# Eight transposes per PSUM tile and one copy out of it, in a rotary-embedding and score kernel

## The chip, the cores and the metric

The kernel runs on one core of one Trainium2 chip. The metric is the device time of one execution in microseconds (us). The engines are PE (matmuls and transposes; PEld is its weight load), DVE (vector), ACT (scalar), POOL, and SP, which here only issues transfers. Sixteen DMA engines (so the profile counts them, and its trace has 16 completions for each of the 112 transfers) move data between HBM and the on-chip memory SBUF. PSUM is the memory that PE writes into (`ps` and `bank` in the profile's rows). The tiles that the kernels take there are of 512 or 1024 float32 numbers per partition; I count them in banks of 512 (2 KB).

## The reference

Two tensors `q` and `k` of shape (16 batches, 512 positions, 16 heads, 64) get a rotary embedding, then all scores are formed per batch and head:

```
q_rot = concat([q1*cos - q2*sin, q1*sin + q2*cos])     # k likewise
scores = einsum('bshd,bthd->bsht', q_rot, k_rot)       # (16, 512, 16, 512) float32
```

The input is 67 MB and the output 268 MB.

## The kernel before

Each batch is cut into four slots of 128 positions (C = 4). DVE applies the rotary embedding in place. PE transposes two heads at a time (HP = 8 blocks of 128x128 per slot), since the matmuls of the scores are written with the head dimension along partitions (64x512 operands in the profile's rows). PE then forms the scores of two heads (`scores(i, p)`, p = 0..7), ACT copies each 128x1024 block from PSUM into a staging buffer, and SP stores one 4 MB staging buffer per slot. I call the eight calls of `scores` for one i, with what is mixed in between them, a round.

The part that the change touches is the transposition. Four transposes fill one bank, one copy empties it, and two banks take turns:

```
ps_s_pool = ctx.enter_context(tc.psum_pool(name="ps_s", bufs=3))   # score tiles, 2 banks each
ps_t_pool = ctx.enter_context(tc.psum_pool(name="ps_t", bufs=2))   # transposes, 1 bank each
...
def transposed(which, n, g, copy):
    bank = ps_t_pool.tile([P, 4, P], fp32, tag="ps_t", name="bank")
    for x in range(4):
        ...                                     # cut: choice of src
        nc.tensor.transpose(bank[:, x, :], src, ident)
    ...                                         # cut: choice of dst in qT or kT
    copy(out=dst, in_=src)
```

In the main part (batches 1 to 15) the query halves are transposed after scores 1 and 3 of a round and copied by DVE, the key halves after scores 5 and 6 and copied by ACT. The first part (batch 0) works on units of four heads, so that scores can begin before a whole batch has been loaded. There the order is: early loads, embedding of unit 0, its transposes and copies, first scores, first 1 MB stores, and after score 3 of rounds 0 and 1 the load of a piece of batch 2:

```
for p in range(HP):
    scores(i, p, st)                            # stores 1 MB after p = 1, 3, 5, 7
    ...                                         # cut
    if p == 3 and i < 2:
        load("kq"[i], 2)
```

## Time and profile before

| | before |
|---|---|
| time, median of 6 runs | 801.9 us (801.0 to 802.9) |
| span of the profiled run | 799.2 us |
| bytes moved | 336.17 MB, 421 GB/s mean |
| queue 1, share of 16 engines' span | 98.4% |
| PE busy | 690.9 us (86%) |
| DVE busy | 544.6 us (68%) |
| ACT busy | 561.8 us (70%) |

The row to look at first is that of the transfer queue, not of PE: a queue that fills 98.4% of the span leaves little for anything else to decide. The 86% of PE is a mean over rounds in which it never pauses and rounds in which its scores wait until a staging buffer has been stored (ACT waits 113.9 us for stores in all, PE's scores 70.9 us for ACT). The prediction below shows how that is read.

This is the timeline of the kernel before around its first score (start, duration, engine, line, operation, count; in brackets the idle time before):

```profile
15.16 5.06 PE L155 MATMUL ps<-kT_t,qT_t 64*128 64x512 f32 x12
15.26 0.59 ACT L142 COPY qT_t<-bank 128x512 f32<-128x512 f32 x1 [0.27 <-PE bank L127]
...
20.03 0.35 SPq L165 DMA_DIRECT2D out_dram<-st  x1
...
23.39 0.34 SPq L165 DMA_DIRECT2D out_dram<-st  x1
23.79 0.49 SPq L79 DMA_DIRECT2D k_sb<-in_k_dram  x1
```

The reader is to see that the first score starts at 15.16 us while the second half of the query copy has not even begun, that two stores are issued, at 20.03 and 23.39 us, and that the load of the keys of batch 2 stands behind them at 23.79.

### The profile page before, as it was taken

What the parts mean: (1) busy time and instruction counts of PE and PEld (TensorE: products, weight loads), DVE (VectorE), ACT (ScalarE), POOL (GpSimd) and SP (SyncE); (2) the same over time, 40 slices, a digit from 0 to 9 for tenths busy, and PEclk for the clock granted to TensorE, in tenths of its full rate; (3) what the DMA queues carried; (4) which work ended last, traced back from release to release, by engine and by line L of the source; (5) the groups of instructions that cost most, each with busy time, mean ns of one, the idle gap of its engine ahead of it and who ended that gap; (6) DMA issues with size and microseconds to landing.
All of it is one profiled execution on the core that took longest, in us unless ns stands there. A gap on an engine that the chain in (4) does not pass through costs nothing.

```text
span 799.2 us, 7712 instructions
## 1 busy us (share of the span) xinstructions
PE 690.9 (86%) x3072; PEld 299.7 (37%) x3072; DVE 544.6 (68%) x516; ACT 561.8 (70%) x647; POOL 0.7 (0%) x6
## 2 busy tenths in 40 slices
PE   4989998997979789797897978979789897889970
PEld 2444443443434334343343433434334343334420
DVE  7999987676858568585684866848668586685300
ACT  3878886776848578585775856768567685667870
POOL 0000000000000000000000000000000000000000
PEclk9999999899989899898998989989899898998995
DMA  9999999999999999999999999999999999998995
GB/s 353 420 426 430 431 416 430 426 433 440 424 438 423 428 435 424 442 425 433 427 433 431 432 431 429 433 433 424 426 428 435 433 402 430 438 426 362 429 422 249
DMA packets 17700, 336.17 MB, mean 421 GB/s; under 512 B 1792, under 2 KB 3072, under 8 KB 4096
## 3 DMA queue, kind: packets, MB, share of 16 engines
q1 hardware_dynamic: 17376, 335.55, 98.4%
q8 instruction: 24, 0.39, 0.2%
q10 hardware_dynamic: 288, 0.13, 0.1%
q14 instruction: 12, 0.10, 0.0%
HBM read 67.24 MB, written 268.44 MB: 420 GB/s over the span
## 4 chain that ended last, share of the span: by engine, by line
DMA 50%; PE 37%; DVE 5%; ACT 4%; issue 1%; ACTq 0%; DVEq 0%
DMA out_dram<-st 49%; PE ps L155 28%; PE bank L127 9%; ACT st L162 4%; DVE part L106 2%; DVE early L111 1%; DVE k_sb L107 1%; DVE k_sb L111 1%; DVE early L107 1%; DMA early<-in_k_dram 1%; DVE kT_t L142 0%; DVE q_sb L107 0%; DVE q_sb L111 0%; ACTq L270 0%; DVE qT_t L142 0%
## 5 line engine op out<-in xcount | busy, mean ns | idle before, releaser
L162 ACT COPY st<-ps 128x1024 f32<-128x1024 f32 x512 | 495.3, 1018 | 202.8 <-DMA out_dram<-st 113.9
L155 PE MATMUL ps<-kT_t,qT_t 64*128 64x512 f32 x2048 | 548.6, 654 | 70.9 <-ACT st L162 70.9
L155 PEld LDWEIGHTS ps<-kT_t,qT_t 64*128 64x128 f32 x2048 | 185.4, 198 | 258.9 <-issue 138.9
L142 DVE COPY qT_t<-bank 128x512 f32<-128x512 f32 x118 | 81.6, 691 | 202.4 <-PE bank L127 202.4
L127 PEld LDWEIGHTS bank<-ident,q_sb 128*128 128x128 f32 x480 | 55.6, 152 | 104.5 <-issue 101.9
L127 PE MATMUL bank<-ident,q_sb 128*128 128x128 f32 x480 | 86.8, 309 | 0.9 <-PE ps L155 0.9
L127 PEld LDWEIGHTS bank<-ident,k_sb 128*128 128x128 f32 x480 | 50.5, 141 | 95.1 <-DVE k_sb L107 38.0
L127 PE MATMUL bank<-ident,k_sb 128*128 128x128 f32 x480 | 78.7, 287 | 1.6 <-DVE qT_t L142 1.2
L142 ACT COPY kT_t<-bank 128x512 f32<-128x512 f32 x122 | 72.4, 597 | 6.2 <-PE bank L127 6.2
L107 DVE TENSOR_TENSOR q_sb<-q_sb,cos_t 128x1024 f32<-128x1024 f32 x60 | 73.5, 1225 | 2.1
L111 DVE TENSOR_TENSOR k_sb<-k_sb,part 128x1024 f32<-128x1024 f32 x60 | 73.5, 1225 | 2.1
L107 DVE TENSOR_TENSOR k_sb<-k_sb,cos_t 128x1024 f32<-128x1024 f32 x60 | 73.5, 1225 | 2.0
L106 DVE TENSOR_TENSOR part<-q_sb,ss_t 128x1024 f32<-128x1024 f32 x60 | 73.5, 1225 | 2.0
L106 DVE TENSOR_TENSOR part<-k_sb,ss_t 128x1024 f32<-128x1024 f32 x60 | 73.0, 1216 | 0.1
L111 DVE TENSOR_TENSOR q_sb<-q_sb,part 128x1024 f32<-128x1024 f32 x60 | 72.9, 1216 | 0.0
L127 PE MATMUL bank<-ident,early 128*128 128x128 f32 x64 | 10.5, 316 | 12.2 <-DVE early L111 10.3
L127 PEld LDWEIGHTS bank<-ident,early 128*128 128x128 f32 x64 | 8.3, 161 | 17.6 <-issue 14.3
L106 DVE TENSOR_TENSOR part<-early,ss_t 128x1024 f32<-128x1024 f32 x8 | 9.8, 1223 | 5.7 <-ACT ss_t L187 5.5
L111 DVE TENSOR_TENSOR early<-early,part 128x512 f32<-128x512 f32 x16 | 10.3, 687 | 0.2
L107 DVE TENSOR_TENSOR early<-early,cos_t 128x1024 f32<-128x1024 f32 x8 | 9.8, 1224 | 0.3
L142 ACT COPY qT_t<-bank 128x512 f32<-128x512 f32 x10 | 5.6, 615 | 3.2 <-PE bank L127 3.2
L142 DVE COPY kT_t<-bank 128x512 f32<-128x512 f32 x6 | 4.1, 685 | 1.3 <-PE bank L127 1.3
(9 smaller groups left out, 2.8 us busy)
## 6 DMA issues: line engine op xcount, KB each, us to landing
out_dram<-st SPq DMA_DIRECT2D x60, 4096.0 KB, 25.0
k_sb<-in_k_dram SPq DMA_DIRECT2D x15, 2048.0 KB, 28.4
q_sb<-in_q_dram SPq DMA_DIRECT2D x15, 2048.0 KB, 27.5
out_dram<-st SPq DMA_DIRECT2D x16, 1024.0 KB, 13.0
early<-in_k_dram SPq DMA_DIRECT2D x1, 1536.0 KB, 9.1
early<-in_q_dram SPq DMA_DIRECT2D x1, 1536.0 KB, 12.3
early<-in_k_dram SPq DMA_DIRECT2D x1, 512.0 KB, 4.7
early<-in_q_dram SPq DMA_DIRECT2D x1, 512.0 KB, 5.4
```

Of the source, the lines that this page charges most:

```text
L106: nc.vector.tensor_tensor(pv, xs, ss, op=mult)
L107: nc.vector.tensor_tensor(xc, xc, cs, op=mult)
L111: nc.vector.tensor_tensor(y, y, z, op=add)
L127: nc.tensor.transpose(bank[:, x, :], src, ident)
L142: copy(out=dst, in_=src)
L155: nc.tensor.matmul(out=po, lhsT=lhs[64 * r : 64 * r + 64, :], rhs=rh, start=True, stop=True)
L162: nc.scalar.copy(out=so, in_=si)
```

## The change

All eight transposes of a slot or unit go into one tile of two banks, which one copy empties. The intent is fewer and larger copies, and fewer switches of PE between transposes and scores (in the kernel before, the first score after transposes took 1.06 us, a further one 0.86). The tiles take eight banks as before (now 3 x 2 + 1 x 2); the price is that there is no second transpose tile any more.

```diff
-    ps_t_pool = ctx.enter_context(tc.psum_pool(name="ps_t", bufs=2))
+    ps_t_pool = ctx.enter_context(tc.psum_pool(name="ps_t", bufs=1))
...
-    def transposed(which, n, g, copy):
-        bank = ps_t_pool.tile([P, 4, P], fp32, tag="ps_t", name="bank")
-        for x in range(4):
+    def transposed(which, n, copy):
+        bank = ps_t_pool.tile([P, HP, P], fp32, tag="ps_t", name="bank")
+        for g in range(HP // C):
+            for x in range(C):
...
         # first part, after the scores of a round's p
-                if p in (0, 1) and i > 0:
+                if p == 0 and i > 0:
...
         # main part
-                tr[1], tr[3] = ("q", i + 1, 0), ("q", i + 1, 1)
+                tr[2] = ("q", i + 1)
...
-                tr[5], tr[6] = ("k", i + C, 0), ("k", i + C, 1)
+                tr[5] = ("k", i + C)
```

More of the change, by code (lines that the diff above doesn't have):

```diff
@@ L116 @@
     qT = {}
-    def transposed(which, n, g, copy):
-        bank = ps_t_pool.tile([P, 4, P], fp32, tag="ps_t", name="bank")
-        for x in range(4):
-            if n < C:
-                src = units[which, n][:, x, P * g : P * (g + 1)]
-            else:
-                src = batches[which, n // C][:, n % C, P * (4 * g + x) : P * (4 * g + x + 1)]
-            nc.tensor.transpose(bank[:, x, :], src, ident)
+    def transposed(which, n, copy):
+        bank = ps_t_pool.tile([P, HP, P], fp32, tag="ps_t", name="bank")
+        for g in range(HP // C):
+            for x in range(C):
+                if n < C:
+                    src = units[which, n][:, x, P * g : P * (g + 1)]
+                else:
+                    src = batches[which, n // C][:, n % C, P * (C * g + x) : P * (C * g + x + 1)]
+                nc.tensor.transpose(bank[:, C * g + x, :], src, ident)
         src = bank
         if which == "q":
-            if n not in qT:
-                qT[n] = qt_pool.tile([P, HP, P], fp32, tag="qT", name="qT_t")
-            dst = qT[n][:, 4 * g : 4 * g + 4, :]
+            qT[n] = qt_pool.tile([P, HP, P], fp32, tag="qT", name="qT_t")
+            dst = qT[n]
         else:
@@ L137, in transposed @@
             if n < C:
-                dst = kT[b][:, 2 * n + g].rearrange("p (t c) -> p t c", c=C)
-                src = bank.rearrange("p c t -> p t c")
+                dst = kT[b][:, 2 * n : 2 * n + 2].rearrange("p g (t c) -> p g t c", c=C)
+                src = bank.rearrange("p (g c) t -> p g t c", c=C)
             else:
-                dst = kT[b][:, 4 * g : 4 * g + 4, P * (n % C) : P * (n % C + 1)]
+                dst = kT[b][:, :, P * (n % C) : P * (n % C + 1)]
         copy(out=dst, in_=src)
@@ L167, in scores @@
             nc.sync.dma_start(o_v[b, i % C], st)
-    def tr_act(which, n):
-        for g in range(2):
-            transposed(which, n, g, nc.scalar.copy)
     def run(ops):
@@ L189 @@
             run(rope(which, 0))
-            tr_act(which, 0)
+            transposed(which, 0, nc.scalar.copy)
         for i in range(C):
@@ L202 @@
                 scores(i, p, st)
-                if p in (0, 1) and i > 0:
+                if p == 0 and i > 0:
                     run(dve[:1])
                     dve = dve[1:]
-                    transposed("k", C + i - 1, p, nc.vector.tensor_copy)
+                    transposed("k", C + i - 1, nc.vector.tensor_copy)
                 if p == 3 and i < 2:
@@ L212 @@
                     dve = dve[m:]
-                    tr_act(*nxt.pop(0))
+                    transposed(*nxt.pop(0), nc.scalar.copy)
             run(dve)
```

## The prediction

> **What bounds the kernel now.** I read the page first, then the table of stretches, then the chain that ended last, then the timeline of single rounds. The page's second part shows a kernel whose transfers never rest:
>
> ```profile
> DMA  9999999999999999999999999999999999998995
> GB/s 353 420 426 430 431 416 430 426 433 440 424 438 423 428 435 424 442 425 433 427 433 431 432 431 429 433 433 424 426 428 435 433 402 430 438 426 362 429 422 249
> q1 hardware_dynamic: 17376, 335.55, 98.4%
> ```
>
> The reader is to see that the mean of the 16 DMA engines is at 90% or more in all slices but two, and that queue 1, which carries the kernel's own data, alone fills 98.4% of 16 engines' span: 0.984 x 799.2 = 786 us of the 799 us. The change moves not one byte of these 335.55 MB. In the middle (150 to 600 us) the stretches give a DMA share of 1.00 at 430 to 431 GB/s, so there is no hole there to fill.
>
> Two holes are left, and they decide whether anything can be won. The table of stretches shows them (the columns are the stretch, PE, weight loads, DVE, ACT, POOL with counts, then granted clock, DMA share, GB/s):
>
> ```profile
> 726.00:728.00 2.00, 2.00 (x12) 0.72 (x8) 1.93 (x3) 1.57 (x3) 0.00 (x0) 0.95 0.53 229
> 728.00:730.00 2.00, 2.00 (x12) 1.11 (x12) 1.97 (x2) 1.71 (x4) 0.00 (x0) 1.00 0.34 147
> 730.00:732.00 2.00, 2.00 (x12) 0.81 (x8) 0.06 (x1) 2.00 (x3) 0.00 (x0) 1.00 0.65 279
> ...
> 788.00:790.00 2.00, 0.00 (x0) 0.00 (x0) 0.00 (x0) 0.00 (x0) 0.00 (x0) 0.50 1.22 524
> 790.00:792.00 2.00, 0.00 (x0) 0.00 (x0) 0.00 (x0) 0.00 (x0) 0.00 (x0) 0.50 0.16 66
> 792.00:794.00 2.00, 0.00 (x0) 0.00 (x0) 0.00 (x0) 0.00 (x0) 0.00 (x0) 0.50 0.04 16
> 794.00:796.00 2.00, 0.00 (x0) 0.00 (x0) 0.00 (x0) 0.00 (x0) 0.00 (x0) 0.50 0.08 33
> 796.00:799.00 3.00, 0.00 (x0) 0.00 (x0) 0.00 (x0) 0.00 (x0) 0.00 (x0) 0.50 0.03 11
> ```
>
> In the last 8 us a share of 0.03 to 0.08 is about 1/16 = 0.0625: one engine of the sixteen still works while fifteen are done. The completion records in the trace (sixteen per transfer) agree: the last store completes on the median engine at 790.97 us and on the last engine at 798.33. This laggard falls behind slowly: its distance to the median is 0.7 us at 20 us, 5 us at 340, 10.3 us at 739. A 4 MB store takes the others 9.7 us from one completion to the next and the laggard 9.95; only the last two stores, after every instruction has been fetched, take it 9.69 and 9.67. So I take the bound to be **the slowest DMA engine**, which seems never to be without work. The hole at 726 to 734 is then that of the fifteen fast engines, which had run 10 us ahead; at 728 the laggard still had two stores to do.
>
> The compute engines are fast enough, by little. A steady round (one 4 MB store, a quarter of each input batch, 4.19 + 1.05 = 5.24 MB) needs 5.24 MB / 430 GB/s = 12.2 us of DMA. The timeline shows a round that no transfer holds up, from one transpose to the same one a round later (552.62 to 562.64 us): 10.02 us of PE, which is its slowest engine. So PE idles about 2 us a round, seen as ACT waiting 113.9 us for stores to free a staging buffer (first row below).
>
> ```profile
> L162 ACT COPY st<-ps 128x1024 f32<-128x1024 f32 x512 | 495.3, 1018 | 202.8 <-DMA out_dram<-st 113.9
> L142 DVE COPY qT_t<-bank 128x512 f32<-128x512 f32 x118 | 81.6, 691 | 202.4 <-PE bank L127 202.4
> L142 ACT COPY kT_t<-bank 128x512 f32<-128x512 f32 x122 | 72.4, 597 | 6.2 <-PE bank L127 6.2
> L107 DVE TENSOR_TENSOR q_sb<-q_sb,cos_t 128x1024 f32<-128x1024 f32 x60 | 73.5, 1225 | 2.1
> ```
>
> [...]
>
> **The change part by part.**
> 1. DVE copies. In the main part 59 rounds each lose two copies of 691 ns for one of 1024 elements. The rotary products have that size, at 1225 ns, and cost 687 ns at 512 elements, so I take 1225. Saved: 2 x 691 - 1225 = 157 ns a round, some 9 us of DVE busy time. It lies beside the DMA: 0 on the path.
> 2. ACT copies. About 66 pairs of 597 ns become 66 single ones of about 1020 ns (the score copy is 1018): 174 ns each, 11 us of ACT busy time, but less in pace, since pairs overlap (two in 1.12 us at 48.79). Also beside the DMA.
> 3. PE. In the round above PE spends 8 scores x 0.86 + 4 x 0.20 + 4 x 0.585 = 10.02 us: a score alone is 0.86 and the first after transposes 1.06, from blocks of one score (1.06) and three (2.78). The first part of the kernel shows eight transposes in a row, 20.15 to 21.18 = 1.03 us. After: 8 x 0.86 + 2 x 0.20 + 2 x 1.03 = 9.34, **0.68 us less a round**. Times 60 it is 41 us of PE, but the round waits for 12.2 us of DMA anyway: 0 on the path.
> 4. The lost second buffer. Key transposes start three scores after the query ones end: 3 x 0.86 + 0.20 = 2.8 us. The DVE copy between takes 1.2 us plus about 0.15 of handover. The other way there are five scores, 4.5 us, against one ACT copy of 1.0 and at most a score copy of 1.0 before it. No wait in the steady part; margin 1.4 us.
> 5. Start. The first key and query copies end about 0.4 us later, and the first score, which needed only half of the query copy (15.16 us), now needs all of it: 1.2 us later. The first store would go out at about 21 us, not 20.03. The loads queued before it keep the DMA engines busy until about 24 (last early load complete at 23.7 on the first engine, 24.9 on the last): hidden.
> 6. Instructions. Some 125 copies and their waits disappear. Queues 8 and 14 carry instructions on the same DMA engines; 12 fetches of queue 14 may become 10 or 11, at 0.31 us each: at most 0.6 us, if they lie on the laggard.
>
> Sum on the path: 0 to -0.6 us, estimated as -0.4.
>
> **The rivals.**
> - *The single tile becomes a wait.* If DVE has the rotary products ahead of the query copy (2.45 us a pair), the key transposes could wait, and PE's round grow from 9.34 towards 11. Against it: DVE waits 202.4 us for the transposes (second row above), so it stands ready before the copy. Even a wait of 1.5 us per round stays under 12.2. It would need over 2.9 us in every round to show; then +10 us or more. I give it 2%.
> - *The shorter PE round pays.* After the last load (681 us) a round only stores 4.19 MB, 9.75 us of DMA against 10.02 of PE, so PE is the bound of the fifteen fast engines and the hole at 726 to 734, worth about 3.7 us (shares of 0.53, 0.34, 0.65, 0.63 over 8 us), could close. That would give 798 to 799, still inside 2%. Against it: the laggard has a backlog through the hole, so closing it only lets the fast engines get further ahead.
> - *A later first store leaves the queue empty*: +1 us at most, by item 5.
> - *Run-to-run drift of the laggard.* The three runs before lie within 1.2 us[...].
>
> **Range and chances.** 802.4 - 0.4 = 802.0 us. Below, 800.0 allows for half of the tail hole; above, 804.0 for a bubble at the start and drift. Faster by over 2% would need 16 us out of transfers that fill the span, slower by 2% a wait of 2.9 us each round: faster 0.01, same 0.97, slower 0.02.
>
> **What would show it.** Right: span within 4 us; DMA share 1.00 in the middle; DVE copies about 1225 ns x59, ACT copies about 1020; an unhindered PE round of about 9.3 us; more idle time of ACT on out_dram<-st than 113.9 us, by some tens of us; again about 1/16 of DMA at the end. Wrong: PE rows of the transposes waiting for the copies by tens of us, a DMA share under 0.95 in the middle, or a span some 4 us shorter with no tail of one engine, which would mean that the laggard is not the bound.

Two passages are cut from this text where marked, a paragraph of general statements and a clause on what may move the slowest engine's end: runs and traces of this case do not show them. No term of the sum is cut. It stays at 0 to -0.6 us, estimated as -0.4: items 1 to 5 count as 0 on the path, and item 6 gives at most 0.6 us (two fetches of 0.31 us; ten of the twelve fetches of queue 14 took 309 ns). That fetches take the place of the kernel's own transfers agrees with the packet records: during the 36 fetches of queues 8 and 14 in the kernel before, 15.1 packets of queue 1 are under way on average, and 16.0 in the mean from 150 to 600 us. The last fetch of that trace starts at 765.7 us.

## The result

| | before | after |
|---|---|---|
| time, median of 6 runs | 801.9 us | 802.78 us (802.4 to 804.3) |
| span of the profiled run | 799.2 us | 801.0 us |
| PE busy | 690.9 us | 651.6 us |
| DVE busy | 544.6 us | 540.9 us |
| ACT busy | 561.8 us | 549.7 us |

The ratio of the fast runs is 1.0016, with a 95% interval of 1.0003 to 1.0029. A ratio is the mean time of one kernel's fast runs over that of the other's of the same rounds, so it is not quite the ratio of the medians. The change is the same within 2%, and if anything slower by about 1 us.

The transfers of the changed kernel, from the page's second and third part:

```profile
DMA  9999999999999999999999999999999999998995
GB/s 352 383 426 437 432 415 429 428 429 443 421 439 423 432 430 421 441 423 433 430 427 434 433 430 427 432 432 433 432 431 430 430 406 438 429 433 358 442 420 224
...
q1 hardware_dynamic: 17376, 335.55, 98.3%
```

The bytes and the share are those of before. One number differs early: the second slice (20 to 40 us) has 383 GB/s where the kernel before had 420.

The groups that answer to those of the prediction, in its order and without the rows between them (busy us, mean ns of one, idle before and its releaser):

```profile
L162 ACT COPY st<-ps 128x1024 f32<-128x1024 f32 x512 | 488.9, 1031 | 209.9 <-DMA out_dram<-st 165.4
L142 DVE COPY qT_t<-bank 128x1024 f32<-128x1024 f32 x59 | 72.3, 1225 | 201.0 <-PE bank L128 201.0
L142 ACT COPY kT_t<-bank 128x1024 f32<-128x1024 f32 x61 | 63.5, 1041 | 11.9 <-PE bank L128 11.9
L107 DVE TENSOR_TENSOR q_sb<-q_sb,cos_t 128x1024 f32<-128x1024 f32 x60 | 73.5, 1225 | 2.1
```

The copies became single ones of the expected size and duration, and what was won on the engines reappears in the first row: ACT waits 165.4 us for stores to free a staging buffer, not 113.9.

The end of the changed kernel, in the table of stretches:

```profile
790.00:792.00 2.00, 0.00 (x0) 0.00 (x0) 0.00 (x0) 0.00 (x0) 0.00 (x0) 0.50 0.42 180
792.00:794.00 2.00, 0.00 (x0) 0.00 (x0) 0.00 (x0) 0.00 (x0) 0.00 (x0) 0.50 0.08 33
794.00:796.00 2.00, 0.00 (x0) 0.00 (x0) 0.00 (x0) 0.00 (x0) 0.00 (x0) 0.50 0.04 16
```

Again about one engine in sixteen works through the last 8 us. The last of the sixteen completions of the last store comes at 800.17 us, 1.84 us later than before; the median one comes at 791.54, not 790.97.

**Where the 1.84 us come from.** I compared the last of the sixteen completions of each transfer, changed against before, one trace of each. (The records don't name the engine; in what follows "the slowest engine" is whichever completes last.) Up to 30 us the difference is 0.2 us or less. At the load of the keys of batch 2 it jumps to +1.54 (36.59 against 35.05). It is +1.2 at 51 us, +2.5 at 189 and +2.2 at 209 us, and from there to the end it moves only between 1.5 and 2.2. So the changed kernel is not slower per round. It lost time in the first 210 us, most of it in one jump near 30 us, and never got it back. The timeline of its start shows what is there:

```profile
15.37 1.01 ACT L142 COPY qT_t<-bank 128x1024 f32<-128x1024 f32 x1 [2.84 <-PE bank L128]
...
16.44 5.39 PE L155 MATMUL ps<-kT_t,qT_t 64*128 64x512 f32 x12 [1.10 <-ACT qT_t L142]
...
21.30 0.35 SPq L165 DMA_DIRECT2D out_dram<-st  x1
...
25.00 0.34 SPq L165 DMA_DIRECT2D out_dram<-st  x1
25.39 0.43 SPq L79 DMA_DIRECT2D k_sb<-in_k_dram  x1
```

The first score waits for the whole query copy and starts 1.28 us later, the first store is issued 1.27 us later, the second (25.00 us) and the load behind it 1.6 us later.

Two rows of stretches of 10 us in the first part, of the kernel before:

```profile
26.00:36.00 10.00, 10.00 (x51) 4.53 (x52) 8.60 (x11) 8.69 (x13) 0.00 (x0) 1.00 1.02 422
36.00:46.00 10.00, 9.11 (x50) 4.54 (x50) 9.83 (x11) 7.57 (x11) 0.00 (x0) 1.00 1.03 435
```

and of the changed kernel:

```profile
26.00:36.00 10.00, 9.19 (x52) 4.71 (x50) 6.27 (x8) 7.96 (x9) 0.00 (x0) 1.00 0.98 348
36.00:46.00 10.00, 8.37 (x44) 3.71 (x42) 9.79 (x11) 8.23 (x9) 0.00 (x0) 1.00 1.02 431
```

The last two columns are the DMA share and GB/s. Between 26 and 36 us the changed kernel's DMA engines count as busy (0.98) but move 348 GB/s, not 422: 74 GB/s over 10 us is 0.74 MB, or 1.7 us at 430 GB/s. So little of this is an empty queue (the share fell by 0.04, 0.4 us of the 10). The packets themselves take longer: in the packet records the 16 KB packets of the key load have a mean of 762 ns in the changed kernel and 634 before, the 8 KB packets of the second store 365 and 310.

### The profile page after: what moved, and what is told of

Same layout as the page of the kernel before. It is cut to its first block, busy times and chain, and to the rows that moved or that the text cites. A ratio compares the mean times of both kernels' runs of the same rounds, so it can differ in the third digit from the quotient of the medians.

```text
span 801.0 us, 7596 instructions
## 1 busy us (share of the span) xinstructions
PE 651.6 (81%) x3072; PEld 309.6 (39%) x3072; DVE 540.9 (68%) x454; ACT 549.7 (69%) x581; POOL 0.7 (0%) x6
## 4 chain that ended last, share of the span: by engine, by line
DMA 59%; PE 19%; ACT 13%; DVE 5%; issue 1%; ACTq 0%
DMA out_dram<-st 59%; PE ps L155 15%; ACT st L162 12%; PE bank L128 4%; DVE part L106 2%; ACT kT_t L142 1%; DVE early L111 1%; DVE k_sb L107 1%; DVE k_sb L111 1%; DVE early L107 1%; DMA sin_t<-in_sin_dram 0%; DVE kT_t L142 0%; DVE q_sb L107 0%; DVE q_sb L111 0%; ACT qT_t L142 0%
## 5 line engine op out<-in xcount | busy, mean ns | idle before, releaser
L162 ACT COPY st<-ps 128x1024 f32<-128x1024 f32 x512 | 488.9, 1031 | 209.9 <-DMA out_dram<-st 165.4
L155 PE MATMUL ps<-kT_t,qT_t 64*128 64x512 f32 x2048 | 522.4, 652 | 110.3 <-ACT st L162 108.8
L155 PEld LDWEIGHTS ps<-kT_t,qT_t 64*128 64x128 f32 x2048 | 196.2, 201 | 347.8 <-ACT st L162 206.3
L142 DVE COPY qT_t<-bank 128x1024 f32<-128x1024 f32 x59 | 72.3, 1225 | 201.0 <-PE bank L128 201.0
L106 DVE TENSOR_TENSOR part<-q_sb,ss_t 128x1024 f32<-128x1024 f32 x60 | 73.5, 1225 | 2.1
L107 DVE TENSOR_TENSOR q_sb<-q_sb,cos_t 128x1024 f32<-128x1024 f32 x60 | 73.5, 1225 | 2.1
L111 DVE TENSOR_TENSOR k_sb<-k_sb,part 128x1024 f32<-128x1024 f32 x60 | 73.5, 1225 | 2.1
L107 DVE TENSOR_TENSOR k_sb<-k_sb,cos_t 128x1024 f32<-128x1024 f32 x60 | 73.5, 1225 | 2.1
L106 DVE TENSOR_TENSOR part<-k_sb,ss_t 128x1024 f32<-128x1024 f32 x60 | 73.5, 1225 | 2.0
L142 ACT COPY kT_t<-bank 128x1024 f32<-128x1024 f32 x61 | 63.5, 1041 | 11.9 <-PE bank L128 11.9
L128 PEld LDWEIGHTS bank<-ident,q_sb 128*128 128x128 f32 x480 | 51.3, 140 | 46.9 <-issue 24.2
L128 PE MATMUL bank<-ident,k_sb 128*128 128x128 f32 x480 | 68.0, 286 | 1.4 <-DVE qT_t L142 1.4
L128 PE MATMUL bank<-ident,q_sb 128*128 128x128 f32 x480 | 65.5, 279 | 1.4 <-issue 1.4
L106 DVE TENSOR_TENSOR part<-early,ss_t 128x1024 f32<-128x1024 f32 x8 | 9.8, 1225 | 5.9 <-ACT ss_t L183 5.6
L111 DVE TENSOR_TENSOR early<-early,part 128x512 f32<-128x512 f32 x16 | 10.3, 687 | 0.2
L142 ACT COPY qT_t<-bank 128x1024 f32<-128x1024 f32 x5 | 5.2, 1032 | 4.3 <-PE bank L128 4.3
L142 DVE COPY kT_t<-bank 128x1024 f32<-128x1024 f32 x3 | 3.7, 1220 | 3.6 <-PE bank L128 3.6
```

The source lines that it names most:

```text
L106: nc.vector.tensor_tensor(pv, xs, ss, op=mult)
L107: nc.vector.tensor_tensor(xc, xc, cs, op=mult)
L111: nc.vector.tensor_tensor(y, y, z, op=add)
L128: nc.tensor.transpose(bank[:, C * g + x, :], src, ident)
L155: nc.tensor.matmul(out=po, lhsT=lhs[64 * r : 64 * r + 64, :], rhs=rh, start=True, stop=True)
L162: nc.scalar.copy(out=so, in_=si)
```

## The experiments

**Theory 1**: the later first score makes the first stores and the load behind them late, this costs transfer time near 30 us, and since the slowest DMA engine is never idle again, the loss stays to the end. **Theory 2**: it is run-to-run drift. **Theory 3**: the single tile makes PE wait in the main part. And apart from the 1 to 2 us: is the gain of 0.68 us a round real and merely hidden?

Medians and ratios, all against runs of the kernel before on the same chip:

| run | median us | before, same chip | ratio | 95% interval |
|---|---|---|---|---|
| after_again | 803.39 | 800.81 | 1.0026 | 1.0012 to 1.0040 |
| start_halves | 802.30 | 800.81 | 1.0017 | 1.0004 to 1.0029 |
| early_loads | 801.39 | 800.81 | 1.0004 | 0.9992 to 1.0017 |
| split_last | 808.78 | 800.81 | 1.0095 | 1.0081 to 1.0109 |
| before_half | 663.39 | 801.60 | 0.8275 | 0.8262 to 0.8288 |
| after_half | 626.85 | 801.60 | 0.7817 | 0.7807 to 0.7828 |
| delay_start | 805.71 | 801.60 | 1.0054 | 1.0041 to 1.0066 |
| delay_middle | 803.06 | 801.60 | 1.0020 | 1.0007 to 1.0033 |
| before_late | 802.26 | 801.55 | 1.0008 | 0.9995 to 1.0020 |
| before_early | 802.50 | 801.55 | 1.0011 | 0.9997 to 1.0024 |

### after_again: the changed kernel once more

No edit.

> The changed kernel itself once more, for a second trace and more rounds. Theory 1 (the later first store opens a hole in the transfers between 27 and 36 us, and an engine that is never idle again carries it to the end): ratio to before 1.001 to 1.003, and the stretch 26 to 36 us again well below 420 GB/s (before: about 420). Theory 2 (run-to-run drift of the slowest DMA engine): the ratio interval holds 1.000, and the stretch 26 to 36 us is as in before.

The ratio is 1.0026 and its interval does not hold 1. The second trace again shows a slow stretch:

```profile
26.00:36.00 10.00, 9.19 (x50) 4.55 (x48) 6.02 (x7) 7.96 (x10) 0.00 (x0) 1.00 1.00 342
```

342 GB/s, with a second store issued at 25.34 us. This speaks against drift alone (theory 2).

### start_halves: only unit 0 copied in two halves again

```diff
-        copy(out=dst, in_=src)
+        if n == 0:
+            for g in range(2):
+                ...                  # cut: copy of half g of the two-bank tile
+        else:
+            copy(out=dst, in_=src)
```

> Only the copies of unit 0 leave in two halves again, everything else as changed. Theory 1: first score at about 15.2 us and first store at about 20.0 instead of 21.3, the hole shrinks from about 1.5 us to under 0.5, time 0.8 to 1.5 us under the changed kernel of the same rounds. Theory 2 (drift) or 3 (waits for the single tile in the main part): no difference to the changed kernel, within 0.5 us.

The stretch from 26 to 36 us rose to 388 GB/s, about half of the way back to 422. But the first store was issued at 20.99 us, not at the expected 20.0, and the second at 23.98, so the lateness was undone only in part, and mostly not by the edit. The first half copy of the query began only after all eight transposes (15.48 us; before: 14.41), so the first score came at 16.12 us, 0.3 us earlier than in the changed kernel, not 1.2. The rest came from PE: the pairs of score matmuls start 0.85 us apart in the first microseconds of every trace and 0.43 later, and the moment of the switch differs between executions. The first three scores took 4.68 us here, 5.39 in the changed kernel, 5.06 in the kernel before, 5.49 in after_again and 3.54 in before_early. So the issue of the second store varies whatever the edit: 24.44 to 25.34 us in the six traces that start as the changed kernel does, 21.86 to 23.39 in the three that start as the kernel before does. The two ranges don't meet, so the lateness is the change's, but its 1.6 us is known to about 1 us only.

The median is 1.1 us under that of the changed kernel of the same rounds, in the expected range, but the two sets of runs overlap (801.55 to 803.32 against 802.71 to 803.75). It points the way of theory 1 without settling it.

### early_loads: the loads of batch 2 ahead of the first store

```diff
         load("k", 1)
         load("q", 1)
+        load("k", 2)
+        load("q", 2)
...
-                if p == 3 and i < 2:
-                    load("kq"[i], 2)
```

> The changed kernel with the loads of batch 2 issued right after those of batch 1, so that 4.19 MB more (9.7 us of DMA) stand in the queue ahead of the first store. Theory 1: no stretch of 2 us between 10 and 40 us under 400 GB/s, time 1 to 2 us under the changed kernel, so about 801. Theory 2 or 3: as the changed kernel within 0.5 us.

```profile
26.00:36.00 10.00, 9.19 (x50) 4.74 (x50) 6.26 (x7) 7.96 (x9) 0.00 (x0) 1.00 0.99 419
```

With 4.19 MB more in the queue the slow stretch is gone (419 GB/s), although the first store is issued no earlier (21.20 us). The packets of the loads take 615 ns. All five runs (801.14 to 802.01) lie under all five of the changed kernel (802.71 to 803.75), 2.0 us by the medians, as expected of theory 1. The changed kernel is then level with the kernel before (ratio 1.0004), not ahead of it.

### delay_start and delay_middle: the same delay early and late

```diff
+        if (i, p) == (0, 0):         # delay_middle: (30, 0)
+            for _ in range(4):
+                nc.scalar.copy(out=so, in_=si)
```

> The changed kernel with the first score copied out five times instead of once, so that the first store goes out about 3.7 us later still. Theory 1: what is lost in the start is never won back, so 3 to 4 us slower than the changed kernel, about 806. Rival (the hole is not due to late stores): within 1 us of the changed kernel.

> The same four extra copies, but in round 30, in the steady part. Theory 1: the queue holds 15 us or more of transfers there, so nothing: within 0.7 us of the changed kernel. Rival (any lost time on the evacuating engine counts): 3 to 4 us slower.

The same four extra copies, some 4 us of ACT, cost clearly more at the start. In delay_start the first store goes out at 24.68 us, and this time the DMA engines do run empty (stretches of 2 us):

```profile
22.00:24.00 2.00, 0.21 (x2) 0.21 (x4) 1.93 (x3) 1.97 (x3) 0.00 (x0) 1.00 0.60 254
24.00:26.00 2.00, 2.00 (x10) 0.69 (x10) 1.97 (x2) 2.00 (x3) 0.00 (x0) 1.00 0.31 131
```

The missing share is 2 x 0.40 + 2 x 0.69 = 2.2 us, and the packets behind are slow as well (356 GB/s from 26 to 36 us). The ratio is 1.0054, against 1.0020 for delay_middle on the same chip: 0.0034 of 802 us is 2.7 us, a little less than the 3 to 4 expected. On the slowest engine the difference to before was 3.4 us at 51 us and 4.3 at the end. In round 30 the same delay leaves the median where the changed kernel's is (ratios 1.0016 and 1.0026 in its two sets of runs). So the same lost time counts more at the start than in a steady round.

Two things in delay_middle do not fit neatly. The expected 15 us of transfers were not in the queue: the extra copies ran from 375.0 to 379.1 us, and when the round's store was issued at 389.1, the transfer ahead of it was complete at 391.6 on the median engine and at 398.6 on the slowest. And its start is the changed kernel's, but in its trace the second store came at 24.44 us (PE's first three scores took 4.54 us) and the slowest engine lost only 0.4 us by 51 us; it ended 2.45 us behind all the same, of which 1.3 was lost between 51 and 209 us and about 0.7 between 407 and 427 us, in the delayed store and the transfers behind it. The start is not the only place where a run can lose time.

### before_late and before_early: the two sides of it in the kernel before

```diff
+        if (i, p) == (0, 0):         # before_late
+            for _ in range(2):
+                nc.scalar.copy(out=so, in_=si)
```

> The kernel before, with nothing changed but two extra copies of the first score (1.8 us on the evacuating engine), so that its second store is issued about as late as in the changed kernel (25 us instead of 23.4). If the late issue is the whole cause: packets of the second store and of the load behind it slow as in the changed kernel (means about 370 and 760 ns instead of 310 and 634), and ratio to before 1.0015 to 1.003. If the cause lies in another part of the change (the single tile, the order in the main part): ratio within 0.001 of 1.

> The kernel before with the loads of batch 2 issued ahead of the first store, as in the run of the changed kernel with early loads. The kernel before had only about 0.3 us per engine of slow packets there, so: 0 to 0.6 us faster, ratio 0.999 to 1.000. If early loads help for another reason than the late stores, they help here as much as in the changed kernel: 2 us, ratio about 0.9975.

before_late missed its aim: the two copies took 2.06 us, but PE's first three scores took 4.09 us in this execution and not 5.06, so the second store moved only to 24.11 us, not to 25. The packets slowed by less accordingly (326 and 692 ns), the stretch from 26 to 36 us fell to 393 GB/s, and the ratio is 1.0008 with 1 inside its interval. The size fits (0.6 us against an excess in the packet times that grew by 0.6 us per engine), but the timing alone proves nothing.

before_early shows that early loads are not a gain in themselves. The kernel before had little to win there, and its ratio is 1.0011, again with 1 inside. Read together with early_loads, this is the best evidence for theory 1: with the loads of batch 2 early, both kernels stand level with the kernel before (1.0011 and 1.0004, on two chips); with the loads where they were, the changed one takes 1.0016 and 1.0026 times its time. In its trace it was 0.65 us ahead at 53 us, 2.0 behind at 209 and 0.8 behind at the end. What costs it time between 51 and 209 us is not explained.

**Lateness against packet time.** The issue times and the packet records of eight of the twelve traces give one table. Lead is the time from the issue of a transfer to its first packet; which packet belongs to which transfer follows from their size and order. The excess is the time that packets from 20 to 45 us took over the usual ones of their size (309 ns for 8 KB, 611 for 16 KB, and so on), per engine.

| run | lead of 2nd store, us | its packets, ns | lead of key load, us | its packets, ns | excess, us |
|---|---|---|---|---|---|
| before | 2.65 | 310 | 4.5 | 634 | 0.27 |
| start_halves | 1.94 | 319 | 3.9 | 706 | 0.90 |
| before_late | 1.78 | 326 | 3.9 | 692 | 0.85 |
| delay_middle | 1.65 | 338 | 3.8 | 694 | 0.95 |
| after | 1.16 | 365 | 3.6 | 762 | 1.72 |
| after_again | 0.85 | 400 | 3.5 | 762 | 2.00 |
| delay_start | 0.84 | 405 | 3.4 | 762 | 2.09 |
| early_loads | 10.8 | 313 | 18.4 | 615 | 0.13 |

In the seven rows above early_loads, the shorter the lead, the slower the packets of the store; with a long lead both transfers run at their usual pace. The four traces left out fit: 2.79 us and 310 ns (before_half), 1.02 and 372 (split_last), 0.89 and 390 (after_half), 13.9 and 310 (before_early). The excess fits the loss too: by 51 us the slowest engine was 0.4 to 0.6 us behind the trace of before in the rows with 0.85 to 0.95, and 1.2 and 2.2 in after and after_again. But the lead alone does not do it: the first store of delay_start also had a lead of 0.84 us, and its packets took 317 ns. The mechanism behind it is not shown by any run.

### before_half and after_half: the transfers taken out of the way

```diff
-            nc.sync.dma_start(o_v[b, i % C], st)
+            nc.sync.dma_start(o_v[b, i % C, :, : H // 2], st[:, : H // 2])
```

Half of each main-part store is left out in both kernels. Their outputs are wrong, which doesn't matter for the times.

> The kernel before with only half the heads of each main-part store written (output wrong on purpose): a steady round then moves 2.10 + 1.05 MB, about 7.3 us at 430 GB/s, so PE with its round of 10.02 us becomes the bound. Theory 1 (the gain on PE is real but hidden behind the transfers): about 75 us of start plus 60 rounds of 10.0 plus the end, some 685 us. If PE is slower than its timeline says: over 710.

> The changed kernel with the same half stores (output wrong on purpose). Theory 1: the round falls by 0.68 us to about 9.34, so 36 to 42 us under the kernel before with half stores, some 645 us. If the single two-bank tile makes PE wait (the rival of the prediction): less than 20 us gained, or slower, and rows of waits of the transposes for the copies of tens of us.

The kernel before now takes 663.4 us (I had expected 685; as the round is the expected 10.02 us, the miss lies in what was allowed for start and end) and the changed one 626.9 (645 expected, the same miss): 36.5 us less, at the low edge of the 36 to 42 expected. In the PE timeline a round of before_half goes from one first query transpose to the next,

```profile
405.51 0.66 PE L127 MATMUL bank<-ident,q_sb 128*128 128x128 f32 x4
...
415.53 0.66 PE L127 MATMUL bank<-ident,q_sb 128*128 128x128 f32 x4
```

10.02 us, and one of after_half likewise,

```profile
405.13 1.09 PE L128 MATMUL bank<-ident,q_sb 128*128 128x128 f32 x8
408.93 1.09 PE L128 MATMUL bank<-ident,k_sb 128*128 128x128 f32 x8
...
414.45 1.09 PE L128 MATMUL bank<-ident,q_sb 128*128 128x128 f32 x8
```

9.32 us. So the gain is real, and it was hidden. This also answers theory 3, at full speed, where the copies have the least time: the key transposes follow the query ones after 3.80 us, with three scores in between, and the waits of the transposes for the copies are few (waited for, us in total, times, longest):

```profile
PEld bank L128 <- DVE qT_t L142: 3.0, 2, 2.2
PEld bank L128 <- ACT kT_t L142: 2.3, 1, 2.3
...
PE bank L128 <- ACT kT_t L142: 1.9, 1, 1.9
...
PE bank L128 <- DVE qT_t L142: 1.4, 1, 1.4
```

Five waits in the whole kernel, four of them before 75 us and the last of 0.8 us. (The answer also has some 110 pauses of 0.8 us, put down to DVE's rotary products. They are the usual pause of the weight load before a group of transposes, while PE is still busy with scores; the kernel before has as many, put down to other instructions.) The second transpose tile was not needed.

### split_last: an attempt at the tail of one engine

```diff
-            nc.sync.dma_start(o_v[b, i % C], st)
+            if i < NST - 1:
+                nc.sync.dma_start(o_v[b, i % C], st)
+            else:
+                nc.sync.dma_start(o_v[b, i % C, 120:], st[120:])
+                nc.sync.dma_start(o_v[b, i % C, :120], st[:120])
```

> The changed kernel with its last 4 MB store cut by partitions into 8 and 120[...]. If one DMA engine is the bound and it is the 16th: time 4 to 7 us lower, about 797, and no tail of some 8 us at 1/16 of the DMA share. If the laggard is another engine: no gain, or 1 to 2 us slower. If no single engine is the bound: within 1 us.

This failed: 808.78 us, 5.4 slower than the changed kernel. The choice of 8 and 120 partitions rested on an assumption of mine about which engines a transfer takes; no run had shown it. What this run's trace shows is the count of completions: 15 for the store of 120 partitions and 8 for that of 8, the rest of the sixteen set at once; which engines they were is not shown. The small store, 0.26 MB on eight engines, was done on them only between 784.9 and 795.2 us, and the large one stood behind it. The cut was slow in itself, so the run says nothing on what a tail of one engine costs. The last of the small store's eight completions came 2.1 us after the slowest engine had finished the store ahead of it (793.1), which suggests that the slowest engine is among those eight. Which one it is stays open.

## Why the prediction was right

The measured 802.78 us lie inside the range of 800 to 804, 0.8 over the predicted 802.0, and "same" was given 0.97. The closeness of the number is in part luck: it was built on 802.4, the median of three runs of the kernel before, while that of six is 801.9, and the sign of the small step was wrong (-0.4 predicted, +1.3 by the ratio 1.0016). By its own steps:

- **The bound** held. The DMA share in the middle stayed at 1.00 to 1.01, the tail of about 1/16 came again, and the start delay and the mid-kernel delay show how it works: most of what the transfers lose early stays lost, and what another engine loses in a steady round costs little (about 0.7 us of 4.1 in the trace of delay_middle). That one engine sets the end is read from completion records; no run could take that engine away (split_last). That it is the same one all along is shown only late: in the trace of before the last of the sixteen is 0.01 to 0.9 us behind the last but one up to 209 us, and 4.6 us or more from 500 us on. There the last completions of the last 150 us are 7.2 to 10.3 us behind the median. One reading of the prediction was not exact: it is not the last two stores alone that take the last engine no longer than the others; those that complete one behind the other between 100 and 198 us take it 9.63 to 9.72 us too, so its lag behind the median, 2.1 us at 198 us, grows steadily only from some 200 us on (5.3 at 348, 10.3 at 739). That instruction fetches make it slow, which the prediction hinted at, was not tested; fetches are among those early stores as well (at 113.6, 146.8 and 174.0 us).
- **DVE and ACT copies** (items 1 and 2): 59 DVE copies at 1225 ns, as said; ACT copies at 1041 and 1032 where 1020 was said. In the main part neither moved the end.
- **PE** (item 3): 9.32 us a round measured where 9.34 was worked out, PE busy down by 39.3 us where 41 was said, and hidden, as said: ACT's wait for stores grew by 51.5 us.
- **The lost buffer** (item 4): no wait in the main part but one of 0.8 us, as said.
- **The shorter round pays at the end** (second rival): the hole after 720 us did not close; 720 to 740 us has 353 GB/s, before 351.
- **Instructions** (item 6): queue 14 has one fetch fewer, 11 instead of 12. The predicted -0.4 us of the sum could not be seen.
- **The start** (item 5) is the step that was mis-sized. It foresaw the first store at about 21 us (21.3) but called the delay hidden because the engines had loads until 24 us; the third rival allowed "+1 us at most". In the first trace the slowest engine had lost 1.2 us by 51 us, in the second 2.2. Two things were left out: the second store and the load behind it also shift, by 1.6 us, and both, issued shortly before their turn, were seen to run slow (365 and 762 ns a packet, before 310 and 634) even though the queue was not empty.

So the sum on the path was about +1 to +2 us instead of -0.4. That the late start is the larger part of it rests on early_loads (2.0 us won back) and delay_start. Why packets slow down after a late issue, and the losses between 51 and 209 us (1.0 us in the changed kernel's trace, 2.6 in that of before_early), stay open.

## What to carry to other kernels

Where the transfers fill the span, as here, a shorter round on the engines won nothing: its 0.68 us turned into longer waits for the buffers that the transfers hold, and showed (36.5 us) only when the transfers were made shorter. In such a kernel look instead at what feeds the queue while it is still short: the merged copy delayed its first consumer by 1.28 us, and time by which the first stores go out late may stay to the end (in delay_start 3.4 us at 51 us, 4.3 at the end). Loads that depend on nothing can go ahead of the first store; here they made good that loss (2.0 us), and were no gain where there was none.
